# Banded attention with the low parts of the keys held twice, one copy over the other

## The chip, the cores and the metric

The kernel runs on one core of a Trainium2 chip. What counts is the device time of one execution in microseconds (us), as the median of several runs. The core has five engines that work side by side, each on its own list of instructions in a fixed order: TensorE (PE; its weight loads are a row of their own, PEld), VectorE (DVE), ScalarE (ACT), GpSimd (POOL) and SyncE (SP, which here only issues DMAs). They wait for each other by semaphores.

## The reference

The kernel computes one layer of a hybrid backbone for 128 prompt tokens and 1024 latent tokens: modulated RMSNorm, one combined input projection, three groups side by side (latent attention, windowed attention, a convolution module), an output projection, and a gated feed-forward part. The change is in the windowed attention alone. There are 4 query heads of 64 channels that share 2 key heads in pairs. Each block of 128 queries sees the blocks before, at and after it, 256 cached context keys, and a sink logit:

```python
def banded_window_attention(q, k, v, kc, vc, sink, scale):
    ...
    s_band = jnp.einsum("bnqhgd,bnkhd->bnhgqk", qb, kb).astype(jnp.float32) * scale
    s_band = jnp.where(valid[None, :, None, None], s_band, NEG)
    s_ctx = jnp.einsum("bnqhgd,bkhd->bnhgqk", qb, kc).astype(jnp.float32) * scale
    s_sink = jnp.broadcast_to(sink.astype(jnp.float32)[None, None, :, :, None, None], s_band.shape[:-1] + (1,))
    p = jax.nn.softmax(jnp.concatenate([s_band, s_ctx, s_sink], axis=-1), axis=-1).astype(v.dtype)
    o = jnp.einsum("bnhgqk,bnkhd->bnqhgd", p[..., :nk], vb) + jnp.einsum("bnhgqk,bkhd->bnqhgd", p[..., nk:nk + L], vc)
```

The 128 prompt tokens attend to themselves only.

## The kernel before

Tokens lie in nine tiles of 128: tile 0 is the prompt, tiles 1 to 8 the latents. The stages follow each other: modulation and norms, the input projection, the window stage, the latent attention, the output projection, the two feed-forward parts. A scheduler that knows estimated durations puts the instructions of each engine into their order; the Python code gives it the sequence to start from.

Products are made from split operands. A number x is held as a high part, rounded to the matmul's format, and a low part, the rest. In the window stage the tile `qst` holds for each query head the high part of its 64 channels in one half of the 128 partitions and the low part in the other. `kHd` holds the high part of the keys of each key head g twice, in both halves, so that one product over 128 rows gives (q high + q low) times k high (L620 and L623). `kLd` holds the low part of the keys once: key head 0 in partitions 0 to 63, key head 1 in 64 to 127. The second product (L621 and L624) takes the half of `qst` with the high parts and the half of `kLd` of its head, so it has 64 active rows. Both add up in the same PSUM bank.

A **window** is one tile t and one key head g; there are 18, in the order of tiles 1 to 8 and then 0. For each of its two query heads `scores` writes a **block** of matmuls: two over the 256 context keys (L620, L621), two over the band of 128 to 384 keys (L623, L624), and one that adds the mask (L627, L629 or L631). Tile 0 has L623 and L624 alone. Then follow, per head, the maximum on VectorE (L636), the exponential on ScalarE (L641), the reciprocal (L646) and the norm on GpSimd (L647). `turn` transposes the probabilities on TensorE (L657), they are split by ScalarE and VectorE (L68, L69) or ScalarE and GpSimd (L587 to L589), and `values` multiplies them (L667). `join` adds the halves up. A plan (SPLAN, L793) weaves the scores of the next window into the turns and values of this one, and a table (SIDE, L784) hangs other work on the windows: rope products (L730), the convolution's norm (`ln_task`, `back_task`), weights, late keys.

The keys come from `put_k` (L450): per key head ScalarE writes the high part, GpSimd copies it to the other half (L454), VectorE writes the low part (L455). It is called for the context and for tiles 1 to 4 before the stage (L497, L499), and for tiles 5 to 8 and 0 inside it (`late`, L571). Before the stage GpSimd also has to make the reciprocal root for the last projected tiles (`rstd_of`, L119 and L122, tile `rs_b`); ScalarE scales with it (L518), and TensorE transposes the result (L533) ahead of the first score block.

The buffers meant below are `kvc` (L561, the cached values), the ring `pt` of 3 for probabilities and raw weights, and the ring `ln` of 5 (L696).

Of the kernel before, what the change touches and what calls it, by code (L numbers as in the profile page):

```python
# [18 lines left out]
P = 128  # L19
# [32 lines left out]
def step_kernel(ctx, tc, i, o):  # L52
    nc = tc.nc
    act, dve, pool, pe, sp = nc.scalar, nc.vector, nc.gpsimd, nc.tensor, nc.sync

    def f(ap):
        return ap.bitcast(F32)
# [56 lines left out]
    def rstd_of(ms, n, more=None, on=pool):  # L114

        t = small.tile([P, 2], F32, name="rs_a", bufs=6)
        r = small.tile([P, 2], F32, name="rs_b", bufs=6)
        if more is None:
            pool.tensor_scalar(t[:, :n], ms, 1.0, EPS, ALU.mult, ALU.add)  # L119
        else:  # L120
            on.tensor_scalar(t[:, :n], ms, more, EPS, ALU.add, ALU.add)
        pool.tensor_tensor(r[:, :n], t[:, :n], expo[:, :n], op=ALU.pow)  # L122
        return r
# [8 lines left out]
    def wtile():  # L132
        return pwork[0].tile([P, 512], F32, name="w")
# [11 lines left out]
    tp = wtile()  # L145
# [4 lines left out]
    tp = wtile()  # L150
# [6 lines left out]
    tp = wtile()  # L157
# [88 lines left out]
    def gtile():  # L246
        return pg.tile([P, 512], F32, name="g")
# [195 lines left out]
    tp = wtile()  # L443
# [3 lines left out]

    ws = [load_w(w_in[:, 2 * j:2 * j + 2, 0:416], 2, 416, pool) for j in range(4)]

    def put_k(sl, tp, n):  # L450
        for g in range(2):
            s = tp[64 * g:64 * g + 64, :n]
            act.copy(kHd[0:64, g, sl], s)
            pool.tensor_scalar(kHd[64:128, g, sl], f(kHd[0:64, g, sl]), 1.0, 0.0, ALU.mult, ALU.add)  # L454
            dve.tensor_sub(kLd[64 * g:64 * g + 64, sl], s, f(kHd[0:64, g, sl]))  # L455

    def put_task(g0, g1, j, alloc=None):
        n, sl = (g1 - g0) * P, slice(g0 * P, g1 * P)
        tp = (alloc or wtile)()
        for t in range(g0, g1):  # L460
            pe.transpose(tp[:, (t - g0) * P:(t - g0 + 1) * P], zs[:, t, j * P:(j + 1) * P], ident)
        if j == 2:
            put_k(sl, tp, n)
        else:
            for h in range(2):
                s = tp[64 * h:64 * h + 64, :n]
                hi, lo = (qst[64 * q:64 * q + 64, 2 * j + h, sl] for q in (j, 1 - j))
                act.copy(hi, s)
                ins = dve.tensor_sub(lo, s, f(hi))
        return ins if j < 2 else None  # L470

    def window_operands():

        nonlocal qst, kHd, kLd, mask, identr, w2h, w2l, wrh, wrl
        ta, tb = (hpa.tile([P, KD * HA], F32R, name=n) for n in ("hHa", "hLa"))

        def cut(t, widths):
            at = 0
            for w in widths:
                yield t[:, at:at + w]  # L480
                at += w

        qst, w2h, wrh = cut(ta, (4 * TOK, 512, 1024))
        kHd, kLd, mask, identr, w2l, wrl = cut(tb, (2 * KALL, KALL, 2 * P, P, 512, 1024))
        qst = qst.rearrange("p (h t) -> p h t", h=4)
        kHd = kHd.rearrange("p (g t) -> p g t", g=2)
        w2h, w2l, wrh, wrl = (x.rearrange("p (k n) -> p k n", k=2) for x in (w2h, w2l, wrh, wrl))
        kc = zp.tile([P, 384], F32, name="zm", bufs=4)[:, 0:256].rearrange("p (t d) -> p t d", t=2)
        sp.dma_start(out=kc, in_=i["kv_c"].rearrange("(t p) d -> p t d", p=P)[:, :, 0:P])
        act.copy(identr, ident)  # L490
        maskf = zp.tile([P, 384], F32, name="zm", bufs=4)[:, 0:2 * P]
        sp.dma_start(out=maskf, in_=i["mask"])
        act.copy(mask, maskf)
        tp = gtile()
        for t in range(2):
            pe.transpose(tp[:, t * P:(t + 1) * P], kc[:, t, :], ident)
        put_k(slice(TOK, KALL), tp, 256)  # L497
        for j in (2, 0, 1):
            ins = put_task(1, 5, j, gtile)  # L499
        marks.append(ins)  # L500

    marks = []
    qst = kHd = kLd = mask = identr = w2h = w2l = wrh = wrl = None
    sink = small.tile([P, 4], F32, name="sink", bufs=1)
    sp.dma_start(out=sink, in_=i["sink"].broadcast_to([P, 4]))

    for g0, g1 in groups:
        n = (g1 - g0) * P
# [21 lines left out]
        for c, (hi, lo) in enumerate(((cqH[:, 0, :], cqL[:, 0, :]), (cqH[:, 1, :], cqL[:, 1, :]), (ckH, ckL))):  # L530
            tp = wtile()
# [23 lines left out]
    sw = mk("sw", stack=sws)  # L555
    swr = mk("swr", bufs=2, stack=sws)
# [1 line left out]
    pacc = mk("pacc", bufs=1, space=PSUM, stack=sws)  # L558
    pss = mk("pss", bufs=2, space=PSUM, stack=sws)
    vst = sw.tile([P, NT + 2, 2, P], F32R, name="vst")  # L560
    kvc = sw.tile([P, 2, P], F32, name="kvc")  # L561
    sp.dma_start(out=kvc, in_=i["kv_c"].rearrange("(t p) d -> p t d", p=P)[:, :, P:2 * P])

    def put_v(t0, t1, src):
        v = src.rearrange("p t (g d) -> p t g d", g=2)
        act.copy(vst[:, t0:t1, :, 0:64], v)
        (dve, pool)[FL["vst"]].tensor_sub(vst[:, t0:t1, :, 64:128], v, f(vst[:, t0:t1, :, 0:64]))

    put_v(NT, NT + 2, kvc)
    put_v(0, NT, zs[:, :, 384:512])  # L570
    late = [lambda g0=g0, g1=g1, j=j: put_task(g0, g1, j) for g0, g1 in ((5, 9), (0, 1)) for j in (2, 0, 1)]  # L571


# [20 lines left out]
    class Window:  # L594
# [16 lines left out]
        def scores(self, h):  # L611
            t, g, c0, c1 = self.t, self.g, self.c0, self.c1
            hd = 2 * g + h
            s = self.s[h] = pss.tile([P, 1024], F32, name="s")
            q = qst[:, hd, t * P:(t + 1) * P]
            lo = slice(64 * g, 64 * g + 64)
            (dve.tensor_copy, act.copy)[FL["sink"]](s[:, c1:c1 + 1], sink[:, hd:hd + 1])
            if t > 0:
                ks = slice(TOK, KALL)
                pe.matmul(s[:, 512:768], q, kHd[:, g, ks], start=True, stop=False)  # L620
                pe.matmul(s[:, 512:768], q[lo], kLd[lo, ks], start=False, stop=True)  # L621
            ks = slice(self.kb, self.kb + self.nb * P)
            pe.matmul(s[:, c0:512], q, kHd[:, g, ks], start=True, stop=False)  # L623
            pe.matmul(s[:, c0:512], q[lo], kLd[lo, ks], start=False, stop=(t == 0))  # L624
            if t > 1 and t < NT - 1:
                edge = s[:, 0:512].rearrange("p (c k) -> p c k", k=P)[:, 1:4:2, :]
                pe.matmul(edge, identr, mask, start=False, stop=True)  # L627
            elif t == 1:
                pe.matmul(s[:, 384:512], identr, mask[:, P:2 * P], start=False, stop=True)  # L629
            elif t == NT - 1:  # L630
                pe.matmul(s[:, c0:c0 + P], identr, mask[:, 0:P], start=False, stop=True)  # L631
# [51 lines left out]
    ln = {}  # L683

    def ln_task(t):

        ys = t * P + (PADC if t else 0)
        tp = wtile()
        for q in range(2):
            pe.transpose(tp[:, q * P:(q + 1) * P], y[q][:, ys:ys + P], ident)  # L690
        bs = small.tile([P, 6], F32, name="bs")
        mv = small.tile([P, 2], F32, name="mv")
        dve.bn_stats(bs, tp[:, 0:256])
        dve.bn_aggr(mv, bs)
        r = rstd_of(mv[:, 1:2], 1)
        ln[t] = swr.tile([P, 256], F32, name="ln", bufs=5)  # L696
        dve.tensor_scalar(ln[t], tp[:, 0:256], mv[:, 0:1], r[:, 0:1], ALU.subtract, ALU.mult)

    def back_task(g0, g1, q):
# [80 lines left out]
    for g0, g1 in ((0, 1), (1, 3), (3, 5), (5, 7), (7, 9)):  # L780
        lns += [lambda t=t: ln_task(t) for t in range(g0, g1)]
        lns += [lambda g0=g0, g1=g1, q=q: back_task(g0, g1, q) for q in range(2)]
# [37 lines left out]
    for g0, g1 in ((1, 5), (5, 9), (9, 11), (0, 1)):  # L820
        n, sl = (g1 - g0) * P, slice(g0 * P, g1 * P)
        tp = wtile()
# [529 lines left out]
    def load_y(fs, c, n):  # L1352

        raw, hi, lo = (part(dt)[:, 0:len(fs) * n].rearrange("p (f n) -> p f n", f=len(fs)) for dt in (F32, F32R, F32R))
        sp.dma_start(out=raw, in_=y_d[fs[0]:fs[-1] + 1, :, c:c + n].rearrange("f p n -> p f n"))
        act.copy(hi, raw)  # L1356
        dve.tensor_sub(lo, raw, f(hi))  # L1357
        return hi, lo
# [41 lines left out]
    for ts, todo in ROUNDS:  # L1400
        acc = {t: pu.tile([P, 1024], F32, name="u") for t in ts}
        left_ = {t: FF for t in ts}
        for fs, now in todo:
            cols = [(t - 1) * P if t else PC for t in now]
            hi, lo = load_y(fs, cols[0], cols[-1] + P - cols[0])
# [87 lines left out]
```

## Time and profile before

| | |
|---|---|
| device time, median of 3 runs | 1689.64 us (1688.91 to 1692.98) |
| profiled execution, own time | 1693.59 us |
| its span, first to last instruction | 1691.8 us |
| TensorE busy, share of span | 1571.4 us, 93% |
| VectorE, ScalarE, GpSimd busy | 1012.6, 739.3, 953.8 us |
| mean granted TensorE clock | 0.959 |

The span is what the trace covers; the own time has 1.8 us more around it. Durations of single instructions are those of this one execution. Matmuls overlap: the time of one is longer than the step from its start to the start of the next, and it is the steps that add up. [...]

### The profile page before, as it was taken

How to read it: one execution, taken by the hardware profiler on the slowest of the kernel's cores; microseconds unless marked ns; L12 is line 12 of the kernel's file. 1: busy time of each engine (PE TensorE's matmuls, PEld its weight loads, DVE VectorE, ACT ScalarE, POOL GpSimd, SP SyncE). 2: the span in 40 equal slices, each digit the busy share in tenths (PEclk: the TensorE clock that was granted, in tenths of full speed). 3: DMA queues.
4: the chain of work that ended last, by engine and by line, in shares of the span. 5: the costliest groups of instructions: out<-in, count | busy, mean ns of one | idle time of the engine just before them, and what ended most of it. 6: DMA issues, size and time to landing. Idle time of an engine off the chain costs nothing.

```text
span 1691.8 us, 24932 instructions
## 1 busy us (share of the span) xinstructions
PE 1571.4 (93%) x9278; PEld 1371.4 (81%) x9278; DVE 1012.6 (60%) x1474; ACT 739.3 (44%) x1458; POOL 953.8 (56%) x978
## 2 busy tenths in 40 slices
PE   6799898998899989798998999999999999999997
PEld 3677585767688878687887999999999998878886
DVE  1679525665677777675349787766777776132222
ACT  2511154565577767663225343333333344242321
POOL 1514955664488788782445597777777753130221
PEclk8899996987899999999998999999999999999999
DMA  9363110214000000306541222222222246344341
GB/s 348 120 230 125 63 36 25 82 55 119 1 23 25 13 27 17 107 1 215 156 161 57 66 71 72 78 79 78 79 78 66 66 142 223 112 143 129 106 150 56
DMA packets 86831, 160.88 MB, mean 95 GB/s; under 512 B 8831, under 2 KB 49063, under 8 KB 86711
## 3 DMA queue, kind: packets, MB, share of 16 engines
q1 hardware_dynamic: 72135, 137.34, 25.1%
q0 software_dynamic: 3552, 12.52, 2.8%
q10 hardware_dynamic: 11024, 9.44, 1.6%
q8 instruction: 73, 1.20, 0.3%
q14 instruction: 47, 0.39, 0.1%
HBM read 124.09 MB, written 34.46 MB: 94 GB/s over the span
## 4 chain that ended last, share of the span: by engine, by line
PE 58%; DVE 7%; ACT 4%; issue 3%; POOL 2%; DMA 0%; ACTq 0%; POOLq 0%; DVEq 0%
PE u L63 14%; PE u L62 14%; PE u L61 14%; PE acc L970 2%; PE w L961 2%; PE po L61 2%; PE po L62 2%; PE po L63 2%; ACT pt L946 2%; PE s L61 1%; DVE mst L939 1%; PE s L62 1%; PE s L63 1%; DVE mst L952 1%; DVE pl L69 1%
## 5 line engine op out<-in xcount | busy, mean ns | idle before, releaser
L1285 POOL TENSOR_TENSOR as<-q,as 128x512 fp32r<-128x512 f32 x100 | 176.2, 1781 | 105.0 <-ACT as L1284 104.9
L1284 ACT CAST as<-q 128x512 fp32r<-128x512 f32 x145 | 88.6, 618 | 206.8 <-PE u L62 177.4
L1318 DVE SCALAR_TENSOR_TENSOR h<-h,fw,h 128x1154 f32<-128x1154 f32 x88 | 159.4, 1816 | 21.3 <-ACT h L1316 19.1
L589 POOL TENSOR_TENSOR pl<-pf,ph 128x512 fp32r<-128x512 f32 x106 | 137.4, 1301 | 3.1
L1357 DVE TENSOR_TENSOR as<-as 128x384 fp32r<-128x384 f32 (+2 forms) x62 | 39.4, 637 | 132.2 <-ACT as L1356 83.8
L961 PE MATMUL w<-ident,pt 128*128 128x128 f32 x640 | 98.6, 281 | 20.1 <-DVE pl L69 13.1
L954 POOL TENSOR_SCALAR pt<-pt,mst 128x1280 f32<-128x1280 f32 x60 | 80.3, 1338 | 38.6 <-DVE mst L953 35.4
L961 PEld LDWEIGHTS w<-ident,pt 128*128 128x128 f32 x640 | 74.9, 143 | 32.1 <-DVE pl L69 17.0
L588 POOL TENSOR_SCALAR ph<-pf 128x512 fp32r<-128x512 f32 x106 | 66.7, 632 | 54.8 <-ACT pf L587 47.1
L538 DVE SCALAR_TENSOR_TENSOR y<-u,cw,y 128x1167 f32<-128x1167 f32 x60 | 94.6, 1593 | 1.1
L1349 POOL TENSOR_TENSOR as<-q,as 128x512 fp32r<-128x512 f32 x18 | 23.0, 1289 | 119.3 <-ACT as L1348 92.8
L1356 ACT CAST as<-as 128x384 fp32r<-128x384 f32 (+2 forms) x62 | 32.9, 533 | 126.2 <-DMA as<-y_d 115.1
L946 ACT ACTIVATE pt<-s,mst 128x1024 f32<-128x1024 f32 x64 | 71.7, 1121 | 28.3 <-DVE mst L941 25.3
L939 DVE TENSOR_REDUCE mst<-s 128x1 f32<-128x1024 f32 x64 | 77.3, 1215 | 11.2 <-PE s L63 10.9
L61 PE MATMUL u<-h,as 128*128 128x290 f32 (+1 forms) x248 | 80.9, 326 | 1.2 <-ACT h L1245 1.2
L62 PE MATMUL u<-h,as 128*128 128x290 f32 (+1 forms) x248 | 80.7, 325 | 0.0
L63 PE MATMUL u<-h,as 128*128 128x290 f32 (+1 forms) x248 | 80.4, 324 | 0.0
L587 ACT COPY pf<-w 128x512 f32<-128x512 f32 x106 | 62.3, 590 | 29.6 <-PE w L961 14.6
L69 DVE TENSOR_TENSOR pl<-w,ph 128x512 fp32r<-128x512 f32 (+1 forms) x104 | 65.9, 638 | 12.9 <-ACT ph L68 11.4
L68 ACT CAST ph<-w 128x512 fp32r<-128x512 f32 (+1 forms) x104 | 56.7, 551 | 31.0 <-PE w L657 13.6
L1316 ACT ACTIVATE h<-h,vec,fw 128x1154 f32<-128x1154 f32 x44 | 59.4, 1353 | 24.2 <-POOL h L1315 13.4
L61 PE MATMUL s<-kT,q 96*128 96x512 f32 x128 | 56.3, 444 | 10.3 <-ACT pt L946 9.6
(546 smaller groups left out, 5621.9 us busy)
## 6 DMA issues: line engine op xcount, KB each, us to landing
q<-in_w_up SPq DMA_DIRECT2D x44, 512.0 KB, 3.5
q<-in_w_down SPq DMA_DIRECT2D x34, 512.0 KB, 3.7
y_d<-h SPq DMA_DIRECT2D x22, 577.0 KB, 5.5
q<-ot_d POOLq DMA_DIRECT2D x18, 512.0 KB, 5.8
as<-y_d SPq DMA_DIRECT2D x44, 192.0 KB, 3.7
adaw<-in_ada_w SPq DMA_DIRECT2D x8, 1024.0 KB, 13.4
cqH<-in_ada_w SPq DMA_DIRECT2D x12, 512.0 KB
adaw<-in_ada_w SPq DMA_DIRECT2D x10, 512.0 KB
```

Source lines behind the costliest of these rows:

```text
L61: pe.matmul(out, lh, rh, start=first, stop=False)
L62: pe.matmul(out, lh, rl, start=False, stop=False)
L63: return pe.matmul(out, ll, rh, start=False, stop=last)
L69: dve.tensor_sub(lo, src, f(hi))
L538: dve.scalar_tensor_tensor(y[q], u[q][:, j:j + CONVN], cw[:, q, j:j + 1], y[q], ALU.mult, ALU.add)
L589: pool.tensor_sub(pl[:, :n], pf[:, :n], f(ph[:, :n]))
L939: dve.tensor_reduce(st[:, 0:1], self.s1[d], op=ALU.max, axis=AX.X, negate=True)
L946: act.activation(pt[:, 0:1024], self.s1[d], AF.Exp, bias=st[:, 2:3], accum_out=st[:, 3:4])
L961: pe.transpose(tp[:, (2 * d + e) * P:(2 * d + e + 1) * P], self.pt[e][:, (2 * c + d) * P:(2 * c + d + 1) * P], ident)
L1284: act.copy(ops[n][0], src)
L1285: (dve if f_ == 0 or n in (1, 4) else pool).tensor_sub(ops[n][1], src, f(ops[n][0]))
L1318: dve.scalar_tensor_tensor(y[:, m], z[:, m, j:j + YW], fw[:, j, v:v + 1], y[:, m], ALU.mult, ALU.add)
```

## The change

The low parts of the keys get both halves of the partitions too, in two tiles, one for each key head: key head 0 keeps the old tile, whose upper half now takes a copy of its lower half, and key head 1 gets a new tile `kL2`. The second products take all 128 rows of `qst` and of their tile, so they add q low times k low as well. The copies are made by GpSimd: at the start of the stage for the context and tiles 1 to 4 (six copies), and in `put_k` for the late tiles (four). To make room `kvc` is taken from the ring `pt`, and `ln` has 2 buffers instead of 5.

```diff
+    def copy_half(to, src, g, sl):
+
+        a, b = slice(64 * g, 64 * g + 64), slice(64 - 64 * g, 128 - 64 * g)
+        pool.tensor_scalar(to[b, sl], f(src[a, sl]), 1.0, 0.0, ALU.mult, ALU.add)
+
-    def put_k(sl, tp, n):
+    def put_k(sl, tp, n, double):
...
-            dve.tensor_sub(kLd[64 * g:64 * g + 64, sl], s, f(kHd[0:64, g, sl]))
+            dve.tensor_sub(kLs[g][64 * g:64 * g + 64, sl], s, f(kHd[0:64, g, sl]))
+            if double:
+                copy_half(kLs[g], kLs[g], g, sl)
...
-    kvc = sw.tile([P, 2, P], F32, name="kvc")
+    kvc = swr.tile([P, 2, 644], F32, name="pt", bufs=3)[:, :, 0:P]
...
+    kL2 = sw.tile([P, KALL], F32R, name="kL2")
+    for sl in (slice(P, 5 * P), slice(TOK, KALL)):
+        copy_half(kL2, kLs[1], 1, sl)
+        pool.tensor_scalar(kL2[64:128, sl], f(kLs[1][64:128, sl]), 1.0, 0.0, ALU.mult, ALU.add)
+        copy_half(kLs[0], kLs[0], 0, sl)
+    kLs[1] = kL2
...
-            lo = slice(64 * g, 64 * g + 64)
...
-                pe.matmul(s[:, 512:768], q[lo], kLd[lo, ks], start=False, stop=True)
+                pe.matmul(s[:, 512:768], q, kLs[g][:, ks], start=False, stop=True)
...
-            pe.matmul(s[:, c0:512], q[lo], kLd[lo, ks], start=False, stop=(t == 0))
+            pe.matmul(s[:, c0:512], q, kLs[g][:, ks], start=False, stop=(t == 0))
...
-        ln[t] = swr.tile([P, 256], F32, name="ln", bufs=5)
+        ln[t] = swr.tile([P, 256], F32, name="ln", bufs=2)
```

The first place where the order changes is on GpSimd just ahead of the stage. Before (`vst` is the split of the values, `rs_b` the reciprocal root, `rot` and `zkr` the rotary part of the latent keys):

```order
L122 TENSOR_TENSOR rs_b<-rs_a,expo 128x2
L567 TENSOR_TENSOR vst<-zs,vst 128x18x64
L119 TENSOR_SCALAR rs_a<-ms 128x2
L398 TENSOR_TENSOR rot_1939<-zkr,ropek 128x32
L404 TENSOR_TENSOR rot_1940<-zkr,ropek 128x8 x4
L567 TENSOR_TENSOR vst<-kvc,vst 128x4x64
L122 TENSOR_TENSOR rs_b<-rs_a,expo 128x2
```

In the changed kernel, at the same place (its line numbers are 8 to 13 higher; `hLa` is the memory in which the old key tile lies, `kL` the new tile):

```order
L122 TENSOR_TENSOR rs_b<-rs_a,expo 128x2
L453 TENSOR_SCALAR kL_2078<-hLa 64x512
L580 TENSOR_SCALAR kL_2078<-hLa 64x512
L453 TENSOR_SCALAR kL_2078<-hLa 64x256
L580 TENSOR_SCALAR kL_2078<-hLa 64x256
L575 TENSOR_TENSOR vst<-zs,vst 128x18x64
L119 TENSOR_SCALAR rs_a<-ms 128x2
L453 TENSOR_SCALAR hLa<-hLa 64x512
L453 TENSOR_SCALAR hLa<-hLa 64x256
L398 TENSOR_TENSOR rot_1939<-zkr,ropek 128x32
L404 TENSOR_TENSOR rot_1940<-zkr,ropek 128x8 x4
L575 TENSOR_TENSOR vst<-pt,vst 128x4x64
```

All six copies stand ahead of the second `rs_b`, which in the changed kernel is the next row. The second place is GpSimd in the first windows, where the keys of tiles 5 to 8 come in. Before (`pt` with `st` is the norm, `ph` and `pl` the split of turned probabilities, `hHa<-pt` a weight):

```order
L647 TENSOR_SCALAR pt<-pt,st 128x512 x2
L454 TENSOR_SCALAR hLa<-hLa 64x512
L647 TENSOR_SCALAR pt<-pt,st 128x512
L712 TENSOR_SCALAR hHa<-pt 128x1024
L454 TENSOR_SCALAR hLa<-hLa 64x512
L588 TENSOR_SCALAR ph<-pf 128x512
L589 TENSOR_TENSOR pl<-pf,ph 128x512
L647 TENSOR_SCALAR pt<-pt,st 128x512
L647 TENSOR_SCALAR pt<-pt,st 128x640
```

And in the changed kernel:

```order
L660 TENSOR_SCALAR pt<-pt,st 128x512 x2
L459 TENSOR_SCALAR hLa<-hLa 64x512
L660 TENSOR_SCALAR pt<-pt,st 128x512
L602 TENSOR_SCALAR ph<-pf 128x512
L725 TENSOR_SCALAR hHa<-pt 128x1024
L453 TENSOR_SCALAR hLa<-hLa 64x512
L603 TENSOR_TENSOR pl<-pf,ph 128x512
L459 TENSOR_SCALAR hLa<-hLa 64x512
L660 TENSOR_SCALAR pt<-pt,st 128x512
L453 TENSOR_SCALAR kL_2078<-kL_2078 64x512
L660 TENSOR_SCALAR pt<-pt,st 128x640
```

Two copies (L453) come in between the norms; the two small ones of tile 0 follow later in the same way. On TensorE the rows keep their order but for two blocks at the start that change places with neighbouring value products.

## Rows read from the trace of the kernel before

**Rows 1.** First part of the page: busy time, share of the span, instructions.

```profile
PE 1571.4 (93%) x9278; PEld 1371.4 (81%) x9278; DVE 1012.6 (60%) x1474; ACT 739.3 (44%) x1458; POOL 953.8 (56%) x978
```

**Rows 2.** Window stage as one stretch: its length, busy time (instructions) by engine.

```profile
core 0: us, PE busy (x) PEld busy (x) DVE busy (x) ACT busy (x) POOL busy (x), PEclk, DMA share, GB/s
257.20:409.40 152.20, 140.94 (x672) 109.09 (x671) 95.57 (x248) 84.58 (x211) 93.61 (x134) 0.82 0.21 64
```

**Rows 3.** Waits in the stage: us in total, times, longest us.

```profile
DVE st L636 <- PE s L627: 17.5, 16, 2.5
...
PEld s L624 <- issue: 6.3, 29, 0.3
...
PE w L533 <- ACT zm L518: 5.2, 1, 5.2
```

**Rows 4.** Timeline of TensorE at the high clock: start us, us, instruction.

```profile
281.66 0.28 PE L620 MATMUL s<-hLa,hHa 128*128 128x256 f32 x1
281.87 0.38 PE L621 MATMUL s<-hLa,hHa 64*128 64x256 f32 x1
282.18 0.44 PE L623 MATMUL s<-hLa,hHa 128*128 128x384 f32 x1
282.55 0.43 PE L624 MATMUL s<-hLa,hHa 64*128 64x384 f32 x1
282.92 0.39 PE L627 MATMUL s<-hLa 128*128 128x256 f32 x1
283.14 0.28 PE L667 MATMUL acc<-pl,vst 128*128 128x256 f32 x1
...
283.38 0.28 PE L667 MATMUL acc<-pl,vst 128*128 128x256 f32 x1
283.50 0.34 PE L61 MATMUL w<-cqH,hHa 128*128 128x384 f32 x1
283.67 0.33 PE L62 MATMUL w<-cqL,hHa 128*128 128x384 f32 x1
```

**Rows 5.** The same view at the lower granted clock.

```profile
293.15 0.55 PE L620 MATMUL s<-hLa,hHa 128*128 128x256 f32 x1 [1.15 <-DVE s L617]
...
295.75 0.41 PE L703 MATMUL w<-ident,ln 128*128 128x128 f32 x1
...
303.39 0.41 PE L667 MATMUL acc<-ph,vst 128*128 128x256 f32 x1
303.60 0.52 PE L61 MATMUL w<-cqH,hHa 128*128 128x384 f32 x1
303.92 0.52 PE L62 MATMUL w<-cqL,hHa 128*128 128x384 f32 x1
```

**Rows 6.** Line L624 alone in four stretches: matmuls (x), weight loads (x), granted clock.

```profile
257.20:275.60 18.40, 3.00 (x5) 1.43 (x5) 0.51 0.00 0
...
288.60:299.20 10.60, 1.81 (x3) 0.75 (x3) 0.52 0.16 53
...
350.60:360.50 9.90, 1.37 (x2) 0.57 (x2) 0.50 0.05 13
...
381.00:394.80 13.80, 2.01 (x4) 1.05 (x4) 0.51 0.13 39
```

**Rows 7.** Groups by line and form: count, busy us, mean ns, idle before.

```profile
L454 POOL TENSOR_SCALAR hLa<-hLa 64x512 fp32r<-64x512 f32 x4 | 2.5, 614 | 3.6 <-ACT hLa L453 3.5
...
L454 POOL TENSOR_SCALAR hLa<-hLa 64x256 fp32r<-64x256 f32 x2 | 0.8, 400 | 3.8 <-ACT hLa L453 3.8
```

**Rows 8.** Timeline of all engines at the stage's start; in brackets the idle time before.

```profile
250.58 2.64 POOL L567 TENSOR_TENSOR vst<-zs,vst 128x1152 fp32r<-128x1152 f32 x1 [0.48 <-ACT vst L566]
...
255.60 0.69 POOL L122 TENSOR_TENSOR rs_b<-rs_a,expo 128x2 f32<-128x2 f32 x1
256.32 0.47 ACT L518 ACTIVATE zm<-g,rs_b 128x256 f32<-128x256 f32 x1 [3.10 <-POOL rs_b L122]
...
256.85 0.69 PE L533 MATMUL w<-ident,zm 128*128 128x128 f32 x2 [5.22 <-ACT zm L518]
...
275.67 0.69 POOL L647 TENSOR_SCALAR pt<-pt,st 128x512 f32<-128x512 f32 x1 [1.78 <-DVE s L617]
```

More of the change, by code (lines that the diff above doesn't have):

```diff
@@ L454, in put_k, with put_task @@
             pool.tensor_scalar(kHd[64:128, g, sl], f(kHd[0:64, g, sl]), 1.0, 0.0, ALU.mult, ALU.add)
-            dve.tensor_sub(kLd[64 * g:64 * g + 64, sl], s, f(kHd[0:64, g, sl]))
-    def put_task(g0, g1, j, alloc=None):
+            dve.tensor_sub(kLs[g][64 * g:64 * g + 64, sl], s, f(kHd[0:64, g, sl]))
+            if double:
+                copy_half(kLs[g], kLs[g], g, sl)
+    def put_task(g0, g1, j, alloc=None, double=True):
         n, sl = (g1 - g0) * P, slice(g0 * P, g1 * P)
@@ L462, in put_task @@
         if j == 2:
-            put_k(sl, tp, n)
+            put_k(sl, tp, n, double)
         else:
@@ L472, in window_operands @@
     def window_operands():
-        nonlocal qst, kHd, kLd, mask, identr, w2h, w2l, wrh, wrl
+        nonlocal qst, kHd, kLs, mask, identr, w2h, w2l, wrh, wrl
         ta, tb = (hpa.tile([P, KD * HA], F32R, name=n) for n in ("hHa", "hLa"))
@@ L483, in window_operands @@
         qst, w2h, wrh = cut(ta, (4 * TOK, 512, 1024))
-        kHd, kLd, mask, identr, w2l, wrl = cut(tb, (2 * KALL, KALL, 2 * P, P, 512, 1024))
+        kHd, kL, mask, identr, w2l, wrl = cut(tb, (2 * KALL, KALL, 2 * P, P, 512, 1024))
         qst = qst.rearrange("p (h t) -> p h t", h=4)
         kHd = kHd.rearrange("p (g t) -> p g t", g=2)
+        kLs = [kL, kL]
         w2h, w2l, wrh, wrl = (x.rearrange("p (k n) -> p k n", k=2) for x in (w2h, w2l, wrh, wrl))
@@ L496, in window_operands @@
             pe.transpose(tp[:, t * P:(t + 1) * P], kc[:, t, :], ident)
-        put_k(slice(TOK, KALL), tp, 256)
+        put_k(slice(TOK, KALL), tp, 256, False)
         for j in (2, 0, 1):
-            ins = put_task(1, 5, j, gtile)
+            ins = put_task(1, 5, j, gtile, False)
         marks.append(ins)
     marks = []
-    qst = kHd = kLd = mask = identr = w2h = w2l = wrh = wrl = None
+    qst = kHd = kLs = mask = identr = w2h = w2l = wrh = wrl = None
     sink = small.tile([P, 4], F32, name="sink", bufs=1)
```

## The prediction

> **What bounds the kernel now.** I read the engines' shares first, then the stage that the change touches, then its waits, then single instructions. Over the whole run TensorE is busy 93% of the span [rows 1], but that share mixes stages, so the stage decides. The window stage runs from the first score product at 257.2 us to the last value products at 409.4 us, 152.2 us. In it TensorE is busy 140.9 us, VectorE 95.6, GpSimd 93.6 and ScalarE 84.6 [rows 2]: TensorE has 11.3 us free, the next engine 56.6. The waits say the same. VectorE stands 17.5 us until the last product of a score block is done [rows 3]; no wait of TensorE inside the stage is near that size. So the stage goes at TensorE's pace, and time taken from TensorE there can come out of the total.
>
> A busy TensorE is not one that multiplies all the time. Look at the starts in one score block at the high clock [rows 4]. The value product at 283.38 (256 columns, 128 rows) is followed 0.12 us later, and the 384-column product at 283.50 after 0.17 us. In the block the five products start at 281.66, 281.87, 282.18, 282.55 and 282.92, and the next instruction at 283.14: steps of 0.21, 0.31, 0.37, 0.37 and 0.22 us, together 1.48 us. At the steps of the 128-row products they would need 3 x 0.12 + 2 x 0.17 = 0.70 us. The excess, 0.78 us, lies in the five steps around the four changes between 128 and 64 rows, about 0.2 us for each change. The weight loads of the 64-row product at L624 stand idle on "issue" 29 times, 6.3 us in all [rows 3]: they are not begun ahead of the matmul. [...]
>
> [...] Four stretches of the stage are granted 0.50 to 0.52; 5 + 3 + 2 + 4 = 14 of the 36 blocks lie in them [rows 6].
>
> **The change part by part.**
> *The second products.* 68 matmuls get 128 rows instead of 64; their number, columns and order hardly change. 32 blocks have five products; the four of the prompt tile have two, and I count those as nothing. Of the 32, 12 run at the lower clock now (two of the 14 belong to the prompt tile): 12 x 1.33 + 20 x 0.78 = 31.6 us of TensorE time. That a product with rows from the new tile costs 0.12 us is not in the trace; the bounds are 0.12 (the same columns from another tile) and the present 0.31, and I take 0.12, the row with 128 rows on both sides.
>
> *Copies before the stage.* Six GpSimd copies are new. The shape is there already: 0.61 us for 64x512, 0.40 us for 64x256 [rows 7]. Four of them stand ahead of the long subtraction that now starts at 250.58, two behind it, all six ahead of the power at 255.60 whose result ScalarE waits for at 256.32, for which TensorE waits 5.2 us until 256.85 [rows 3, 8]. This is the path to the first score product. 3 x 0.61 + 3 x 0.40 = 3.0 us, of which the 0.48 us that GpSimd is idle before 250.58 are free: +2.6 us. Two of the copies stay in their own lanes; the nearest row is the same 0.61, and as bounds I keep 0 and the 2.64 us of the big subtraction.
>
> *Copies inside the stage.* The keys of the tiles that come late add two 64x512 and two 64x128 copies (each under 0.40), at most 2.0 us, between the norms of the first units, behind which the turns of the weights wait. GpSimd has 1.78 us idle before the norm at 275.67 [rows 8], so the cost is between 0 and 2.0. In the first three units six blocks give back 5 x 1.33 + 0.78 = 7.4 us, but there the chain over VectorE, ScalarE and GpSimd is long and GpSimd has the copies in its way. I let these units repay the 2.6 us and no more: net 0 by unit 3, with bounds of +4.6 (nothing regained) and -2.8 (all regained).
>
> *Two buffers and the value cache.* The normalised rows of the convolution get 2 buffers instead of 5, and the cache values borrow a buffer of the weights ring. In the new order each pair of rows is turned back before the next is written, and VectorE's instruction there waits for the same engines as before; the borrowed buffer is read before the first unit. I cost both at 0; the cover is the order, and if it failed, VectorE, with 56 us free, would stand behind one pair of turns.
>
> *What is left of the gain.* From unit 3 on the blocks hold 31.6 - 7.4 = 24.2 us. When TensorE gets ahead, each unit's loop (scores, maximum, exponential, norm, turn) becomes late next, and part of the saving turns into waits for GpSimd or ScalarE. GpSimd would have 98 us of work in a stage of some 134, still a quarter free. The ends are all of it, 24, and a third, 8; I take three quarters, 18, nearer the upper end because TensorE is busy 93% of the stage now and its neighbours wait for it.
>
> **Sum.** The profiled execution took 1693.59 us, 1691.8 of span and 1.8 around it. 1693.6 - 18 + 0 = 1675.6. It lies 3.95 us above the median of the three timed runs, 1689.64, so the forecast for the median is 1672.
>
> **The clock** is the other unknown. The four slow stretches are 18.4 + 10.6 + 9.9 + 13.8 = 52.7 us long [rows 6]; I take 51 us of them as work (some waits are in them, as at 293.15 [rows 5]). At the high level it would take 51 / 1.8 = 28 us (1.8 from 2.60 / 1.48), so the stage's work is 90 + 28 = 118 us at the high level, and 118 - 32 x 0.78 = 93 us after the change. With a share c of it at the lower level the stage lasts 93 x (1 + 0.8c) + waits + 2.6. Today c is 28/118 = 0.24.
>
> **Rivals.**
> 1. *The high clock holds longer.* The products come denser, so some of the falls inside the stage don't happen. The fall at 288.6 followed a wait; the one at 350.6 came among score blocks. With c = 0.1 and waits doubled to 22 us: 100 + 22 + 2.6 = 125, 27 less than 152: 1662.
> 2. *The loop takes the saving.* A third of the 24 us survives and the late copies cost their 2.0, the early ones 2.6: -8 + 4.6 = -3.4, 1686. For it: GpSimd and VectorE each have over 93 us of work in strict order. Against: they wait for TensorE now.
> 3. *The change doesn't do what it says:* the excess in the block comes from something other than the row count (the reload of the same queries, the bank), and the steps stay. Then only the copies show: +2.6 to +4.6, 1693. [...] Against it: the value and rope products beside the block step by their columns alone [rows 4], and the excess sits at the changes.
> 4. *Slower: the clock falls.* TensorE waits more between blocks, from unit 3 on, and is granted 0.5 for most of the stage. Each us of work then costs 0.8 us more. With 11 us of waits the stage is as long as today at 93 x (1 + 0.8c) = 152 - 13.6, c = 0.6; at c = 0.7 it is 93 x 1.56 + 13.6 = 158.7, +6.5: 1696. For it: granted clock already falls in four stretches of a stage in which TensorE is 93% busy. Against it: c would have to more than double while the same columns come in less time.
>
> **How the numbers follow.** Forecast 0.60 (its own range 1664 to 1681), rival 1 0.14, rival 2 0.14, rival 3 0.06, rival 4 0.06. A measurement of this kernel can tell about 0.3%, 5.1 us, from no change. Faster than 1684.6: 0.60 + 0.14 + half of rival 2 = 0.81. Within it: the other half, most of rival 3 and a little of rival 4, 0.13. Slower: 0.06. The range 1660 to 1687 leaves out the lower half of rival 1 and rivals 3 and 4, some 0.19.
>
> **What the profile after would show.** Right: blocks of 0.70 to 0.8 us at the high clock with steps of 0.12 and 0.17; the weight loads of the second products begun ahead; the first score product 2 to 3 us later than 257.2 behind a later power; the stage 130 to 138 us long with TensorE's busy time down by some 30 and its waits up. Wrong: blocks still of 1.48 us (rival 3), blocks of 0.7 with the stage no shorter than 145 us and TensorE waiting for GpSimd or ScalarE (rival 2), or a stage granted 0.5 for more than half of its work (rival 4).

## The result, and the profile after

The changed kernel takes 1673.65 us (median of 5 runs, 1670.43 to 1675.06) where the kernel before takes 1689.64: 0.9899 times as long, 95% interval 0.9883 to 0.9915, so 16.0 us less. Two later samples of the same kernel gave 0.9880 and 0.9870 (e5 and e12 below). The profiled execution took 1671.38 us (span 1669.4), 22.2 us less than the profiled one of before; 6.2 us of that is where the two executions lie in their samples, one 3.95 us above its median, the other 2.27 below.

The first part of the page of the changed kernel, to be read against [rows 1]:

```profile
PE 1536.8 (92%) x9278; PEld 1357.1 (81%) x9278; DVE 1014.7 (61%) x1474; ACT 738.0 (44%) x1458; POOL 960.9 (58%) x988
```

The number of matmuls is the same, 9278. TensorE is busy 34.6 us less, GpSimd has ten instructions and 7 us more. The stage as one stretch, from its first score product to its last value product, columns as in [rows 2]:

```profile
261.40:385.40 124.00, 103.92 (x671) 92.74 (x671) 94.36 (x248) 83.39 (x211) 97.27 (x137) 0.92 0.27 83
```

It is 28.2 us shorter than before. TensorE's busy time fell by 37.0 us, its free time rose from 11.3 to 20.1. The granted clock rose from 0.82 to 0.92. One block at the high clock, answering to [rows 4] (its lines are now L633, L634, L636, L637, L640):

```profile
282.80 0.28 PE L633 MATMUL s<-hLa,hHa 128*128 128x256 f32 x1
282.92 0.28 PE L634 MATMUL s<-kL,hHa 128*128 128x256 f32 x1
283.04 0.34 PE L636 MATMUL s<-hLa,hHa 128*128 128x384 f32 x1
283.21 0.34 PE L637 MATMUL s<-kL,hHa 128*128 128x384 f32 x1
283.39 0.28 PE L640 MATMUL s<-hLa 128*128 128x256 f32 x1
283.51 0.28 PE L680 MATMUL acc<-pl,vst 128*128 128x256 f32 x1
```

Subtract starts: steps of 0.12, 0.12, 0.17, 0.18 and 0.12 us, together 0.71 where they were 1.48. And at the lower clock, answering to [rows 5]:

```profile
291.41 0.55 PE L633 MATMUL s<-hLa,hHa 128*128 128x256 f32 x1 [1.15 <-DVE s L630]
291.76 0.41 PE L634 MATMUL s<-kL,hHa 128*128 128x256 f32 x1
...
292.61 0.41 PE L640 MATMUL s<-hLa 128*128 128x256 f32 x1
292.83 0.41 PE L716 MATMUL w<-ident,ln 128*128 128x128 f32 x1
```

1.42 us instead of 2.60; its first step, 0.35, follows a wait. Waits in the stage (us in total, times, longest), to be read against [rows 3]:

```profile
PE w L541 <- ACT zm L526: 8.0, 1, 8.0
...
PE acc L680 <- ACT ph L68: 4.6, 4, 2.8
...
DVE st L649 <- PE s L640: 2.9, 6, 1.0
PEld s L633 <- issue: 2.7, 4, 2.1
```

VectorE's 17.5 us behind the last product of a block have become 2.9, and the second products (now L637) no longer stand among the weight loads on "issue". In exchange TensorE waits for the engines that feed the values. The first row is the price at the start. Timeline of all engines there, to be read against [rows 8]:

```profile
244.93 0.41 ACT L501 CAST hLa<-zm 128x256 fp32r<-128x256 f32 x1 [1.95 <-DMA zm<-in_mask]
...
251.61 0.61 POOL L453 TENSOR_SCALAR kL<-hLa 64x512 fp32r<-64x512 f32 x1
...
253.91 2.69 POOL L575 TENSOR_TENSOR vst<-zs,vst 128x1152 fp32r<-128x1152 f32 x1
...
254.48 2.67 DVE L77 TENSOR_TENSOR hLa<-pf,hHa 128x512 fp32r<-128x512 f32 x1 [0.55 <-ACT hHa L76]
...
259.87 0.69 POOL L122 TENSOR_TENSOR rs_b<-rs_a,expo 128x2 f32<-128x2 f32 x1
...
260.59 0.47 ACT L526 ACTIVATE zm<-g,rs_b 128x256 f32<-128x256 f32 x1 [6.15 <-POOL rs_b L122]
...
261.12 0.69 PE L541 MATMUL w<-ident,zm 128*128 128x128 f32 x2 [8.04 <-ACT zm L526]
```

The power `rs_b` starts at 259.87 instead of 255.60, and the first score product follows at 261.46 instead of 257.19: 4.3 us later. 2.85 us of this are the copies: from the power before (249.40 before, 250.82 now) to this one it is 6.20 us before and 9.05 now. The other 1.4 us came earlier: ScalarE waited 1.95 us for the DMA of the mask, and that wait differs between executions of this one kernel (0.7 us in e5, 1.6 in e12; 0.2 in e1). Whether the change has a part in it stays open. The sum of the two profiles: 28.2 shorter in the stage, less 4.3 at its start, less 2.1 between the stage and the first score product of the latent attention (402.31 instead of 424.07), is 21.8, near the 22.2 of the whole.

### The profile page after: what moved, and what is told of

The parts are those of the page before. It is cut to its first block, busy times and chain, and to the rows that moved or that the text cites. A ratio compares the mean times of both kernels' runs of the same rounds, so it can differ in the third digit from the quotient of the medians.

```text
span 1669.4 us, 24952 instructions
## 1 busy us (share of the span) xinstructions
PE 1536.8 (92%) x9278; PEld 1357.1 (81%) x9278; DVE 1014.7 (61%) x1474; ACT 738.0 (44%) x1458; POOL 960.9 (58%) x988
## 3 DMA queue, kind: packets, MB, share of 16 engines
q1 hardware_dynamic: 72135, 137.34, 25.2%
## 4 chain that ended last, share of the span: by engine, by line
PE 58%; DVE 7%; ACT 3%; issue 3%; POOL 2%; DMA 0%; ACTq 0%; DVEq 0%; POOLq 0%
PE u L63 14%; PE u L62 14%; PE u L61 14%; PE acc L983 3%; PE w L974 2%; PE po L61 2%; PE po L62 2%; PE po L63 2%; ACT pt L959 1%; PE s L61 1%; PE s L62 1%; PE s L63 1%; DVE mst L952 1%; DVE mst L965 1%; DVE pl L69 1%
## 5 line engine op out<-in xcount | busy, mean ns | idle before, releaser
L974 PE MATMUL w<-ident,pt 128*128 128x128 f32 x640 | 99.7, 283 | 20.1 <-DVE pl L69 13.3
L974 PEld LDWEIGHTS w<-ident,pt 128*128 128x128 f32 x640 | 75.8, 144 | 32.5 <-DVE pl L69 17.0
L952 DVE TENSOR_REDUCE mst<-s 128x1 f32<-128x1024 f32 x64 | 77.4, 1216 | 12.8 <-PE s L63 12.6
L959 ACT ACTIVATE pt<-s,mst 128x1024 f32<-128x1024 f32 x64 | 71.6, 1119 | 28.5 <-DVE mst L954 25.6
L69 DVE TENSOR_TENSOR pl<-w,ph 128x512 fp32r<-128x512 f32 (+1 forms) x104 | 65.8, 638 | 11.3 <-ACT ph L68 10.4
## 6 DMA issues: line engine op xcount, KB each, us to landing
adaw<-in_ada_w SPq DMA_DIRECT2D x8, 1024.0 KB, 13.5
```

The lines of the kernel that those rows point to most:

```text
L69: dve.tensor_sub(lo, src, f(hi))
L952: dve.tensor_reduce(st[:, 0:1], self.s1[d], op=ALU.max, axis=AX.X, negate=True)
L959: act.activation(pt[:, 0:1024], self.s1[d], AF.Exp, bias=st[:, 2:3], accum_out=st[:, 3:4])
L974: pe.transpose(tp[:, (2 * d + e) * P:(2 * d + e + 1) * P], self.pt[e][:, (2 * c + d) * P:(2 * c + d + 1) * P], ident)
```

## The experiments

Theory A: TensorE loses about 0.2 us whenever the number of active rows changes between 128 and 64, and making the rows alike is the whole gain; the copies cost a little. Rival B: the block was long for another reason, and the gain comes from the rings, the copies or the new order. "Before" was timed again beside each group: 1690.54, 1692.85, 1689.53, 1693.23 us, in this order.

| kernel | us, median (lowest to highest) | ratio to before, 95% | first score at | stage, us | of it at low clock |
|---|---|---|---|---|---|
| before | 1689.64 | 1 | 257.2 | 152.2 | 55.7 |
| changed | 1673.65 (1670.43-1675.06) | 0.9883-0.9915 | 261.5 | 124.0 | 20.3 |
| e1 | 1702.64 (1694.08-1707.87) | 1.0033-1.0080 | 260.0 | 156.1 | 59.8 |
| e2 | 1679.92 (1673.94-1682.31) | 0.9900-0.9954 | 258.7 | 141.2 | 48.3 |
| e3 | 1687.13 (1680.24-1688.61) | 0.9946-0.9988 | 263.5 | 137.3 | 33.6 |
| e4 | 1672.93 (1672.68-1673.37) | 0.9842-0.9922 | 261.6 | 125.1 | 25.2 |
| e5 | 1673.89 (1671.98-1675.50) | 0.9853-0.9908 | 260.8 | 125.4 | 25.2 |
| e6 | 1691.65 (1687.69-1697.99) | 0.9973-1.0009 | 257.6 | 146.6 | 42.0 |
| e7 | 1665.77 (1663.21-1667.91) | 0.9809-0.9857 | 257.4 | 121.4 | 14.0 |
| e8 | 1663.16 (1661.98-1667.16) | 0.9800-0.9850 | 256.3 | 121.6 | 10.9 |
| e9 | 1669.98 (1666.34-1671.63) | 0.9845-0.9905 | 261.6 | 121.5 | 11.2 |
| e10 | 1666.79 (1664.17-1670.16) | 0.9825-0.9881 | 259.2 | 124.3 | 24.2 |
| e11 | 1675.74 (1673.07-1677.19) | 0.9859-0.9911 | 260.2 | 129.8 | 32.5 |
| e12 | 1672.67 (1672.26-1674.34) | 0.9847-0.9894 | 263.2 | 124.1 | 20.4 |

The last column is worked out from stretches of 2 us: length times (1 - granted clock) times 2, added up. It takes the low level as 0.5 and the high one as 1.00: in the kernel before, 25 of the 77 stretches read 0.50 or 0.51 and 44 read 1.00; the 8 between are counted as means over both. It and the two before it are of one profiled execution each.

**e1: the copies without the products.** The products take 64 rows again; copies and buffers stay.

```diff
-                pe.matmul(s[:, 512:768], q, kLs[g][:, ks], start=False, stop=True)
+                pe.matmul(s[:, 512:768], q[64 * g:64 * g + 64], kLs[g][64 * g:64 * g + 64, ks], start=False, stop=True)
```

(L637 in the same way.) Expected:

> All of the change but the products: the ten copies, the second key tile and the smaller rings stay, the second products take 64 rows again. Theory A (every step between 128 and 64 rows costs TensorE about 0.2 us, the rest of the change only costs): blocks at 1.48 to 1.57 us at the high clock, first score product 2.6 us or more later, total 1692 to 1695. Theory C (the gain came from the new order or the rings): near 1674 with blocks of 1.5 us.

Measured: 12 us slower than before by the medians; the ratio, 1.0056, makes it 9.5 us, with 5.6 to 13.5 as its interval. The gain goes, so it hangs on the rows; the copies cost more than either theory had. The stage of this kernel (the last 1.3 us of this stretch lie behind its last value product):

```profile
260.00:417.50 157.50, 143.13 (x671) 109.61 (x669) 96.09 (x250) 84.99 (x212) 97.67 (x138) 0.81 0.22 67
```

TensorE is as busy as in [rows 2], the clock as low.

**e2: the kernel before, with fewer changes.** No copy, no new rows: the same five products in the order 128, 128, 128 (mask), 64, 64.

```diff
+                pe.matmul(s[:, 512:768], q, kHd[:, g, kc], start=True, stop=False)
             pe.matmul(s[:, c0:512], q, kHd[:, g, ks], start=True, stop=False)
...
+            if t > 0:
+                pe.matmul(s[:, 512:768], q[lo], kLd[lo, kc], start=False, stop=True)
+            pe.matmul(s[:, c0:512], q[lo], kLd[lo, ks], start=False, stop=True)
```

Expected:

> The kernel before, with the products of a block in another order: the three with 128 rows first, then the two with 64 rows. Same products, same rows, no copies; two steps between row counts per block instead of four. Theory A: the block at the high clock goes from 1.48 to about 1.1 us, TensorE gives up some 32 x 0.4 = 13 us, three quarters of it come out: 1678 to 1682. Theory B (a product with 64 rows is slow by itself, or what counts is the number of active rows): the block keeps 1.48 us and the total 1690.

Measured: as theory A had it, 10.6 us faster with no row more. One block at the high clock (start, us, instruction; L625 is the mask):

```profile
283.87 0.28 PE L621 MATMUL s<-hLa,hHa 128*128 128x256 f32 x1
283.99 0.33 PE L622 MATMUL s<-hLa,hHa 128*128 128x384 f32 x1
284.16 0.28 PE L625 MATMUL s<-hLa 128*128 128x256 f32 x1
284.37 0.38 PE L631 MATMUL s<-hLa,hHa 64*128 64x256 f32 x1
284.59 0.33 PE L632 MATMUL s<-hLa,hHa 64*128 64x384 f32 x1
284.85 0.39 PE L668 MATMUL acc<-pl,vst 128*128 128x256 f32 x1
285.07 0.28 PE L668 MATMUL acc<-ph,vst 128*128 128x256 f32 x1
```

Steps 0.12, 0.17, 0.21, 0.22, 0.26 and 0.22. The products of 64 rows are not slow in themselves, since between the two of them nothing is added: each change adds 0.1 us to the step before it and 0.1 us to the step after it. With that rule the five steps of [rows 4] come out too: 0.12 + 0.1, 0.12 + 0.2, 0.17 + 0.2, 0.17 + 0.2, 0.12 + 0.1.

**e3: half of the change.** The context products (L634) take 128 rows, the band products (L637) 64.

```diff
-            pe.matmul(s[:, c0:512], q, kLs[g][:, ks], start=False, stop=(t == 0))
+            pe.matmul(s[:, c0:512], q[64 * g:64 * g + 64], kLs[g][64 * g:64 * g + 64, ks], start=False, stop=(t == 0))
```

Expected:

> The changed kernel with one of the two second products per block back at 64 rows (the band), the context one at 128. Two steps between row counts per block, copies as in the change. Theory A: blocks of about 1.1 us at the high clock as in e2_two_steps though half of the low products have twice the rows, total about 3 to 4 us above e2_two_steps for the copies: 1681 to 1686. Theory B (rows count, not steps): blocks nearer to 0.9 to 1.0, clearly shorter than in e2_two_steps.

Measured: a little above what was expected, between before and the change. The block:

```profile
288.88 0.28 PE L633 MATMUL s<-hLa,hHa 128*128 128x256 f32 x1
289.00 0.28 PE L634 MATMUL s<-kL,hHa 128*128 128x256 f32 x1
289.11 0.34 PE L636 MATMUL s<-hLa,hHa 128*128 128x384 f32 x1
289.38 0.44 PE L637 MATMUL s<-kL,hHa 64*128 64x384 f32 x1
289.75 0.38 PE L640 MATMUL s<-hLa 128*128 128x256 f32 x1
289.97 0.28 PE L680 MATMUL acc<-pl,vst 128*128 128x256 f32 x1
```

0.12, 0.11, 0.27, 0.37, 0.22: 1.09 us with two changes, 0.71 + 2 x 0.2. The weight loads show where the time goes. Those of the block in [rows 4], in the kernel before:

```profile
281.55 0.19 PEld L620 LDWEIGHTS s<-hLa,hHa 128*128 128x128 f32 x1
281.87 0.18 PEld L621 LDWEIGHTS s<-hLa,hHa 64*128 64x128 f32 x1
282.18 0.19 PEld L623 LDWEIGHTS s<-hLa,hHa 128*128 128x128 f32 x1
282.55 0.18 PEld L624 LDWEIGHTS s<-hLa,hHa 64*128 64x128 f32 x1 [0.18 <-issue]
282.92 0.19 PEld L627 LDWEIGHTS s<-hLa 128*128 128x128 f32 x1 [0.18 <-issue]
283.02 0.19 PEld L667 LDWEIGHTS acc<-pl,vst 128*128 128x128 f32 x1
```

Those of L620 and L667 start 0.11 and 0.12 us ahead of their matmuls (281.66 and 283.14); the four behind a change, of L621, L623, L624 and L627, start with theirs. In the block of the changed kernel above, those of L633, L634, L636, L637 and L640 start at 282.69, 282.81, 282.93, 283.05 and 283.22, all 0.11 to 0.17 us ahead. So in these blocks the load behind a change is not begun ahead, whichever way the change goes: two of the four have 128 rows (L623 and L627).

e3 has as many changes as e2, and the copies and buffers besides. It is 7.2 us slower than e2 on the same chip: a second sign that the copies cost more than nothing.

**e4: 96 rows.** The second products of key head 0 take 96 rows.

```diff
-                pe.matmul(s[:, 512:768], q, kLs[g][:, ks], start=False, stop=True)
+                r = slice(0, 96 if g == 0 else P)
+                pe.matmul(s[:, 512:768], q[r], kLs[g][r, ks], start=False, stop=True)
```

(The band product in the same way.) Theory A expects all blocks alike at 0.70 to 0.80 us and 1670 to 1676 us in all; that 96 rows would count as 128 was the author's supposition. Expected:

> The changed kernel with 96 active rows in the second products of key head 0 and 128 in those of key head 1 (a part of the smallest terms is left out, so the result is not the reference's). [...] Theory B (active rows set time or clock): blocks of key head 0 longer than those of key head 1 by 0.1 us or more, and a lower mean clock, total 1676 to 1682.

Measured: the time of the change. A block of key head 0 (L642 is the mask):

```profile
286.54 0.28 PE L633 MATMUL s<-hLa,hHa 128*128 128x256 f32 x1
286.65 0.28 PE L635 MATMUL s<-hLa,hHa 96*128 96x256 f32 x1
286.77 0.34 PE L637 MATMUL s<-hLa,hHa 128*128 128x384 f32 x1
286.95 0.34 PE L639 MATMUL s<-hLa,hHa 96*128 96x384 f32 x1
287.12 0.28 PE L642 MATMUL s<-hLa 128*128 128x256 f32 x1
287.24 0.38 PE L705 MATMUL w<-ident,y 128*128 128x128 f32 x2
```

96 beside 128 steps like 128 beside 128, with steps of 0.11, 0.12, 0.18, 0.17 and 0.12, together 0.70 us. So it is not any difference in rows that costs; of the two tried, 96 and 64 beside 128, only 64 does.

**e5, e6, e7, e8: what the copies and the rings cost.** e5 is the changed kernel once more. e6 has 64-row products and no copies, but the new tile and the smaller rings. e7 makes the six early copies on VectorE:

```diff
-        copy_half(kL2, kLs[1], 1, sl)
-        pool.tensor_scalar(kL2[64:128, sl], f(kLs[1][64:128, sl]), 1.0, 0.0, ALU.mult, ALU.add)
-        copy_half(kLs[0], kLs[0], 0, sl)
+        dve.tensor_copy(kL2[0:64, sl], f(kLs[1][64:128, sl]))
+        dve.tensor_copy(kL2[64:128, sl], f(kLs[1][64:128, sl]))
+        dve.tensor_copy(kLs[0][64:128, sl], f(kLs[0][0:64, sl]))
```

e8 makes the four late ones on ScalarE as well (`act.copy` in `copy_half`). Expected, in the order e5 to e8:

> The changed kernel itself, once more, as the scale for the three others on the same chip: 1670 to 1676, first score product at 260 to 262 us, low granted clock for some 20 us of the window stage if that is a property of the kernel (theory: dense products keep the clock up) and for up to 50 us if the profiled execution was only lucky.

> Products with 64 rows and no copy at all: of the change only the second key tile's place, the ring of 2 and the borrowed buffer stay. Theory A (the buffers cost nothing; what e1_copies_only lost is the copies): 1689 to 1692, as before. Rival: the smaller rings or the moved memory cost what e1_copies_only lost, 1697 to 1703.

> The change with its six copies before the stage on VectorE, which stands idle there from about 250 to 262 us, and the four late ones still on GpSimd. Theory A (the early copies stand on the path to the first score product): first score product about 3 us earlier than in the changed kernel, total 1668 to 1672. Rival (the first windows wait for other things anyway): first score product earlier, but the end of the stage where it was, 1672 to 1675.

> As e7_early_copies_dve, and the four late copies on ScalarE, so GpSimd has no copy of the low parts. If the late copies on GpSimd hold the norms of the first windows back: 2 us below e7_early_copies_dve. If they are hidden there: the same as e7_early_copies_dve, or up to 2 us more because ScalarE has the exponentials in strict order.

Measured: the tile and the rings cost nothing that the total shows (e6: 1.2 us below before, interval 4.6 us below to 1.5 above). The traces do show something: from the last value product to the first score product of the latent attention it takes 14.6 and 14.8 us in the two kernels with the old buffers (before, e2) and 16.1 to 17.1 in the twelve with the new ones, e6 among them. What makes these some 2 us was not tested. e7 is 8.1 us faster than e5, more than expected; e8 another 2.6, within what the samples overlap. The first score product of e5, then of e7:

```profile
260.75 0.56 PE L633 MATMUL s<-hLa,hHa 128*128 128x256 f32 x1
```

```profile
257.39 0.56 PE L633 MATMUL s<-hLa,hHa 128*128 128x256 f32 x1
```

3.4 us of the 8.1 are there before the stage begins. Some of that is where the two executions stood before the copies. The two powers `rs_b` on GpSimd, first those of e5, then those of e7, take this out:

```profile
250.18 0.70 POOL L122 TENSOR_TENSOR rs_b<-rs_a,expo 128x2 f32<-128x2 f32 x1
...
259.16 0.69 POOL L122 TENSOR_TENSOR rs_b<-rs_a,expo 128x2 f32<-128x2 f32 x1
```

```profile
249.65 0.96 POOL L122 TENSOR_TENSOR rs_b<-rs_a,expo 128x2 f32<-128x2 f32 x1
...
255.35 1.13 POOL L122 TENSOR_TENSOR rs_b<-rs_a,expo 128x2 f32<-128x2 f32 x1
```

From the first power to the first score product it is 10.57 us in e5 and 7.74 in e7: 2.8 us for the copies in GpSimd's queue. For the others, the windows 264 to 306 us of e5 and of e7 (columns as in [rows 2]):

```profile
264.00:306.00 42.00, 33.30 (x174) 29.84 (x175) 30.64 (x74) 22.56 (x57) 28.64 (x39) 0.78 0.12 34
```

```profile
264.00:306.00 42.00, 32.31 (x206) 27.44 (x206) 33.92 (x84) 25.30 (x63) 33.02 (x46) 0.99 0.17 51
```

Both stretches lie wholly in the stage. e7's TensorE does 206 matmuls there instead of 174, at a granted clock of 0.99 instead of 0.78. That looked like a second price of the copies, so the next runs test it.

**e9, e10: the length of the copies alone.** e9 is e8 with six GpSimd instructions of the same shapes in the old place, that write rows of the keys back onto themselves (together they took 3.6 us, the copies 3.0); e10 is e8 again.

```diff
+        for kx in (kL2[0:64, sl], kL2[64:128, sl], kLs[0][64:128, sl]):
+            pool.tensor_scalar(kx, f(kx), 1.0, 0.0, ALU.mult, ALU.add)
```

Expected:

> The version without copies on GpSimd (early ones on VectorE, late ones on ScalarE; 1663.2 us before), and with six more GpSimd instructions at the place of the early copies that write rows of the keys back onto themselves: the work and the place of the early copies without their use. Six by 0.61 and 0.40 us: 3.0 us in the queue ahead of the power. Theory A (what costs is GpSimd's queue ahead of the first score product, and beyond its own 3 us a late start brings falls of the clock in the first windows): first score product 3 to 3.5 us later, 1666 to 1672 us, low granted clock again in some stretch between 273 and 297 us. Rival B (what the early copies cost beyond 3 us comes from the late copies standing in GpSimd's queue, which this version does not have): 1666 to 1667 us and the clock at 1.00 from 265 us on.

> The version without copies on GpSimd once more, to be compared with the filler on the same chip: 1662 to 1667 us by both theories, first score product near 256.3 to 257.4 us, granted clock 1.00 from about 265 us to 306 us as in its first profile.

Measured: the filler costs 3.2 us in the medians, about its own length, with samples that overlap. From the first power to the first score product it is 10.84 us in e9 and 7.73 in e10, 3.1 more. That a late start brings the falls of the clock does not hold in the traces: e9, whose first score product comes at 261.6, has 11.2 us at the low clock. e10, the same kernel as e8, was expected to start near 257 and to keep the high clock; it starts at 259.2, 2.9 us later than e8, and has 24.2 us at the low one. The windows 264 to 306 us of e8, then of e10:

```profile
264.00:306.00 42.00, 32.57 (x206) 27.28 (x205) 33.29 (x83) 27.38 (x68) 31.22 (x42) 1.00 0.17 51
```

```profile
264.00:306.00 42.00, 34.07 (x191) 29.33 (x190) 33.04 (x78) 25.30 (x61) 29.13 (x38) 0.85 0.16 47
```

One program, two executions, 0.15 of the clock apart. So a difference of this size between the low stretches of two profiles can't be put down to an edit.

**e11, e12: the late copies alone.** e11 is the change with its early copies on GpSimd and the four late ones on ScalarE; e12 is the change a third time.

```diff
-                copy_half(kLs[g], kLs[g], g, sl)
+                act.copy(kLs[g][b, sl], f(kLs[g][a, sl]))
```

Expected:

> The changed kernel with its early copies on GpSimd as they are, and the four late ones on ScalarE. So far: early copies taken to VectorE gained 8.1 us, the late ones then taken to ScalarE 2.6 more, but GpSimd instructions of the early copies' length cost only 3.2 us in the version without late copies on GpSimd. Theory A (the early copies cost about 3 us, their own length, and the late ones 5 to 8 when the stage starts late, because the norms and splits of the first windows stand behind them): 1666 to 1669 us where the changed kernel has 1673.5. Rival B (the early copies cost 8 us by themselves and the late ones some 2.6): 1670 to 1672 us. The first score product stays near 260.5 us by both.

> The changed kernel once more, beside the version with the late copies on ScalarE on the same chip: 1672 to 1675 us by both theories, 2 to 8 us above that version. In its trace the granted clock falls to 0.5 in some stretch between 270 and 297 us, as in its two profiles so far, if that belongs to this kernel; if it comes and goes with the execution, as in the two profiles of the version without copies on GpSimd, it may be away.

Measured: both theories missed. e12 ran in the time expected, and its clock fell as in the two profiles before (near 273, 280 and 290 us). Taking the late copies off GpSimd made the kernel 3.1 us slower here (1675.74 against 1672.67; the samples, 1673.07 to 1677.19 and 1672.26 to 1674.34, overlap), and it made e7 2.6 us faster. The late copies' place has no price that these runs tell from nothing.

What stays open: the copies cost 3.2 us by the filler, 8.1 by e7, and 11 by e1 beside e6 (1.0056 against 0.9991 of before). About 3 us are shown, with their mechanism. The other 5 to 8 are measured as totals, and no run isolates what makes them.

The table narrows it down, by an estimate. With the prediction's factor of 1.8 (2.60 us for a block at the low clock, 295.75 - 293.15 in [rows 5], over the 1.48 at the high one), a microsecond at the low clock holds 0.56 us of work at the high one, so 0.44 us of each come off. The stages are then 127.7, 128.1 and 129.8 us with four changes in a block (before, e6, e1), 119.9 and 122.5 with two (e2, e3), and 113.7 to 116.8 with none (the nine others), whether GpSimd makes the copies or not. So in these profiles what the copies cost beyond their 3 us lies mostly in the time at the low clock (25.2 us in e5, 14.0 in e7; 59.8 in e1, 42.0 in e6). Whether the copies bring it, or another order of the first windows, or neither, stays open: each run was profiled once, and e8 and e10 differ by 13.3 us of low clock with no edit.

## Why the prediction was right

The time, 1672 forecast, 1673.65 measured, came out by the mechanism that was named. That it came out so closely is luck: two terms of the sum were mis-sized, in opposite directions, and cancelled.

- *What bounds the stage.* Right. Time taken from TensorE came out of the total; e2 shows it without any copy (10.6 us).
- *About 0.2 us for each change of rows.* Right, in three orders: four changes 1.48 us, two 1.09 (e3) and 0.98 with 0.1 more in the step behind (e2), none 0.71. A block with 96 rows beside 128 has no excess (0.70 in e4). Forecast was 0.70, and at the low clock 1.27, from the steps of 0.21 and 0.32 us in [rows 5] (3 x 0.21 + 2 x 0.32), where 1.42 was found behind a wait. The 1.33 us that the forecast counts for each block at that clock are the 2.60 us of [rows 5] less this 1.27; with the 1.42 they are 1.18. Between the two 64-row products of e2 nothing is added, so nothing there shows a 64-row product to be slow in itself. The prediction's remark that the load of L624 is not begun ahead holds in the block of [rows 4] for all four loads behind a change, of 64 rows and of 128.
- *"Three quarters, 18" of 24.2 us.* Too small in the total. The same copies and rings with 64 and with full rows are e1 and e4: 1702.64 and 1672.93 on one chip, 29.7 us. Without copies on GpSimd it is e6 and e8, 1691.65 and 1663.16, 28.5. But these differences hold a change of the clock, which the sum had at nothing: e1 has 59.8 us at the low clock and e4 25.2, some 15 us by the 0.44 above. At one clock the stage lost about 12.6 us (127.7 to 115.1), half of the 32 x 0.78 = 25 us that the changes cost at the high one.
- *The loop of rival 2* took its part: TensorE's free time in the stage went from 11.3 to 20.1 us. What made up for it is the clock of rival 1: low stretches of 55.7 us before (the prediction counted 52.7 in four, and left out a fifth, near 303 us) and 20.3 after. The prediction's own formula gives TensorE 93 x (1 + 0.8 x 0.12) = 102 us with c = 20.3 / 1.8 / 93 = 0.12, where 103.9 were found; with the old c of 0.24 it gives 111. So 8.8 us more of waits and some 9 us less from a smaller share at the low clock stand against each other. That denser products bring the higher clock is argued, not shown: within one kernel the low time went from 10.9 to 24.2 us. Over the kernels with all second products at 64 rows it was 42.0 to 59.8 us, over those with none at 64 it was 10.9 to 32.5, which speaks for it.
- *The stage, "130 to 138 us".* Missed: 124.0, by the clock as above (an estimate from one profiled execution).
- *Early copies "+2.6"* to the first score product: right in size (2.85 in the profiles of before and after, 2.8 in e5 against e7; 3.2 in the total by the filler). *"Net 0 by unit 3"* was the step that failed: e1, which has the copies and repays nothing, lost 9.5 to 12 us (interval from 5.6), beyond the upper bound of 4.6, and e7 gains 8.1 us by having the early ones on VectorE. What makes the part beyond the 3 us of the queue stays open.
- *Rings and borrowed buffer at 0.* Right within e6's interval; some 2 us behind the stage, in every trace with the new buffers, were not foreseen.
- Rival 4, the falling clock, did not come: 0.92 in the stage.

In sum, 18 + 0 was forecast; about 28 gained, by the rows and by the clock together, and 8 to 11 lost were measured.

## What to carry to other kernels

Look in a stream of products for steps that are longer than their columns (here 0.12 us for 256 and 0.17 for 384, at the high clock): where 64-row products stand among 128-row ones, put them side by side, which costs no memory and no copy (e2, 10.6 us), or give all of them 128 rows if the memory is there (16 us). Copies that such a change needs belong on an engine whose queue does not hold the next stage's first step: with the early ones on VectorE the kernel ran in 1663.16 to 1666.79 us in three samples (e7, e8, e10; 0.9825 to 0.9853 of before), the fastest versions here. Before a few microseconds of a stage are put down to an edit, profile the same kernel twice, since the time at the low clock in one kernel's stage moved by 13 us without any edit.

## What the runs showed of the hardware

- 96 active rows among 128 cost nothing (a block of 0.70 us in e4, 0.71 in the changed kernel), 64 among 128 cost 0.1 us in the step on each side of a change, at the high clock (e2, e3 and [rows 4]). In the block of [rows 4] the weight load behind a change starts with its matmul, the others 0.11 and 0.12 us ahead of it.
- The granted clock of one and the same program differed between executions: 1.00 (e8) and 0.85 (e10) over the same 42 us.
- In the changed kernel a VectorE instruction beside a long GpSimd one took 2.67 us (L77 at 254.48, above), and it ends at 257.15, after GpSimd's subtraction at 256.60. In the kernel before, the same instruction began when GpSimd's subtraction had ended (253.22, from [rows 8]) and took 0.69:

```profile
253.25 0.69 DVE L77 TENSOR_TENSOR hLa<-pf,hHa 128x512 fp32r<-128x512 f32 x1 [0.53 <-ACT hHa L76]
```

In e5 it took 2.46 us from 253.97, again beside GpSimd's subtraction (253.27 to 255.88). But in the kernel before another VectorE instruction stood wholly beside GpSimd's subtraction (250.58 to 253.22) and took 0.69, on 64 partitions where L77 has 128:

```profile
252.03 0.69 DVE L469 TENSOR_TENSOR hHa<-g,hHa 64x512 fp32r<-64x512 f32 x1 [2.51 <-ACT hHa L468]
```

So L77 took 2.0 and 1.8 us more where it ran beside GpSimd's subtraction, and what makes the difference is not shown. The 2.0 us did not reach the first score product, which waited for GpSimd's power.
